# A two-layer hybrid trunk: the FFN up projection by seven quarter products, weight sums partly by accumulating DMAs, SBUF pools per sub-layer, adaLN sums moved

## The chip, the cores and the metric

The kernel runs on one core of a Trainium2 chip. TensorE (PE) multiplies, VectorE (DVE) and ScalarE (ACT) do element-wise work, GpSimd (POOL) a little, and SyncE (SP) issues the DMAs. The metric is device time in microseconds of one execution, as the median of repeated runs. A profile is one execution taken by the hardware profiler; its engines' busy times, waits and order of events are what this document reads.

## The reference

Two layers, each with a token mixer and a feed-forward part, over 512 latent and 128 context tokens that share the weights. What matters here is the feed-forward half of a layer (D_MODEL 1024, D_FF 2816), and the adaLN modulation that feeds both halves:

```python
def adaln(cvec, w_mod, b_mod):
    m = jax.nn.silu(cvec) @ w_mod + b_mod
    return jnp.split(m[:, None, :], 6, axis=-1)

def conv_glu(h, w_up, conv, w_down):
    u, val = jnp.split(h @ w_up, 2, axis=-1)
    u = dwconv3(u, conv)
    return (jax.nn.gelu(u, approximate=True) * val) @ w_down

def trunk_layer(...):
    sh1, sc1, gt1, sh2, sc2, gt2 = mod
    ...
    h = rmsnorm(x, g2n) * (1 + sc2) + sh2
    x = x + gt2 * conv_glu(h, w_up, f_conv, w_down)
```

The outputs are the normed tokens of both groups and the keys and values of every layer.

## The kernel before

All activations lie with channels on the 128 partitions and the 640 tokens along the free axis, as two halves of 320 (256 latent and 64 context tokens each). Every large product is taken in float32r with both operands split in two: a high part that ScalarE casts and a low part that VectorE makes by subtraction (`split`, and `block` for weights, lines 114 to 129 and 148 to 150). A product then is high times high, high times low and low times high: three matmuls per 128 channels and half of the tokens (`gemm`, line 136).

`block` loads a weight block of 128 x 1024 (512 KB) through SyncE's queue into one of three `raw` buffers, and writes its parts into one of two `hi`/`lo` pairs, or into spare tiles. PSUM gives out pairs of banks (`mmps`): two of tag `mm` and one of tag `m3`, so three products can be in flight.

`feed_forward` (line 591) runs over 22 units per layer, in two parts of 11. A unit f takes 48 matmuls for its gate block, evacuates them to a padded tile, convolves it with three taps (`dwconv`: one ScalarE and two VectorE instructions, lines 293 to 295), applies GELU, takes 48 matmuls for its value block, multiplies (line 616) and splits the result. After a part the down projection (`project`) adds its share to the residual x, eight blocks of 66 products per half each. Units 0 to 2 lead: `leading` multiplies the first half of the tokens for three blocks before the second half, while `norm` (line 240) still makes the second half's operands.

The adaLN sums are taken on VectorE: `mod_block` (line 162) loads two pieces of 256 KB of `w_mod`, multiplies each by both conditions with an accumulator output (line 171) and adds them up (line 173). 24 of these blocks go beside the branch projections of layer 0, one after each of 24 steps, and 56 beside the FFN of layer 0, two after a unit (`aside`, which only places them behind another instruction).

A list scheduler of the framework sets the order on each engine when the program is built; each engine then works its queue strictly in that order, and waits by semaphores. Pools with a fixed number of buffers per tag make later users wait for earlier ones.

Of the kernel before, what the change touches and what calls it, by code (L numbers as in the profile page):

```python
# [37 lines left out]
KSPARE = (4, 4, 3)  # L38
FTAGS = [("yc", 8)] + [("g", 2)] * 2 + [("vm", 9)] * 9 + [("qk", 10)] * 10
# [6 lines left out]
PARTS = ((0, 11), (11, 22))  # L46
KSPLIT = (6, 5)
# [7 lines left out]
def hybrid_kernel(ctx: ExitStack, tc: tile.TileContext, a):  # L55
# [3 lines left out]
    wp = ctx.enter_context(tc.tile_pool(name="wp", bufs=1))  # L59
    act = ctx.enter_context(tc.tile_pool(name="act", bufs=1))  # L60
# [22 lines left out]

    count = [0]
# [3 lines left out]
    fturn = [0]  # L88
# [5 lines left out]

    def big(tag, bufs, dt=F32):
        return act.tile([P, N], dt, tag=tag, bufs=bufs, name=uid(tag))

    def tmp(dt=F32, width=N):
        t = act.tile([P, PPW], dt, tag="tmp", bufs=NTMP, name=uid("tmp"))
# [14 lines left out]
    def block(src, n=1024, spare=None):  # L114
        """spare: places (first column, end, tag and bufs of both parts) for when the rotating ones are all held."""
        raw = wp.tile([P, 1024], F32, tag="raw", bufs=NRAW, name=uid("raw"))
        nc.sync.dma_start(raw[:, :n], src)
        parts = []
        if spare is None:
            hi = wp.tile([P, 1024], F32R, tag="hi", bufs=NW, name=uid("hi"))  # L120
            lo = wp.tile([P, 1024], F32R, tag="lo", bufs=NW, name=uid("lo"))
            parts.append((0, n, hi, lo))
# [30 lines left out]
    def load_cond():  # L153
        out = []
        for name in ("c", "c_ctx"):
            t = act.tile([P, 1152], F32, tag="bm", bufs=2, name=uid("cond"))[:, :D]
# [5 lines left out]
    def mod_block(l, i, cond):  # L162
        acc = sm.tile([P, 2, 2], F32, tag="macc", name=uid("macc"))
        for hf in range(2):
            turn[0] += 1
            tag, w = (("pt", 768), ("kc", 512), ("pt", 768), ("vca", 512))[turn[0] % 4]
            raw = act.tile([P, w], F32, tag=tag, bufs=2 if tag == "pt" else 1, name=uid("mraw"))[:, :512]
            nc.sync.dma_start(raw, a["w_mod"][l, i, :, hf * 512:(hf + 1) * 512])
            for s in range(2):
                scr = big("yt", 1)  # L170
# [25 lines left out]
    def rsqrt(st, v, r, t):  # L196
        """r = 1 / sqrt(st / D + EPS), with a Newton step"""
# [7 lines left out]
    def rstd(x, c, n=1):  # L205
        """1 / rms of the tokens of n halves from c on, the same on all partitions: one PSUM bank per half."""
# [17 lines left out]
    def half_tiles(n=2):  # L224
        t = act.tile([P, 768], F32, tag="pt", bufs=2, name=uid("xr"))
# [43 lines left out]
    def leading(n, src, h):  # L269
        """The first products after a norm: each half of the tokens for n blocks before the next half."""  # L270
# [95 lines left out]
    def softmax(s_ps, w, bias):  # L366
        s = act.tile([P, 384], F32, tag="s", bufs=4, name=uid("s"))
# [13 lines left out]
    def attention(l, qs, ks, vb, vc):  # L381
        kc = act.tile([P, 512], F32, tag="kc", bufs=1, name=uid("kc"))
        nc.sync.dma_start(kc, a["kc"][l].rearrange("p t n -> p (t n)"))
        vca = act.tile([P, 512], F32, tag="vca", bufs=1, name=uid("vca"))
# [4 lines left out]
        def behind(ins):  # L389
            """The products with V of the unit before: TensorE comes to them a little later than they could start."""  # L390
# [4 lines left out]
        def unit(t, j, bms):  # L395
            pt = act.tile([P, 768], F32, tag="pt", bufs=2, name=uid("pt")).rearrange("p (b e q) -> p b e q", b=3, e=2)
# [33 lines left out]
        def context(t):  # L430
            pt = act.tile([P, 768], F32, tag="pt", bufs=2, name=uid("pt")).rearrange("p (b e q) -> p b e q", b=3, e=2)
# [22 lines left out]
        for t in range(4):  # L454
            bms = []
            for e in range(2):
                bm = act.tile([P, 1152], F32, tag="bm", bufs=2, name=uid("bm")).rearrange("p (v n) -> p v n", v=3)
# [63 lines left out]
    def aside(ins, side, n):  # L521
        """The next n pieces of work that nothing waits for yet, behind ins."""
# [6 lines left out]
    def branch(l, b, h, ys, merged, last=False, side=[], between=None):  # L529
        parts = []  # L530
        for mp in range(4):
            if between:
                between(mp)
            for mi in range(2):
# [18 lines left out]
                aside(ins, side, 1)  # L553
        return parts

# [10 lines left out]
    def project(l, x, get, part, xt, n_last, side=[]):  # L566
        """x += gate * (W^T xt); the last n_last blocks finish one half of the tokens before the other."""
        for m in range(KD - n_last):
            ps = mmps()
            gemm(ps, get(m), xt)  # L570
            aside(residual(l, x, ps, m, part), side, 2)
# [12 lines left out]
    def ffn_block(src, n=1024):  # L584
        fturn[0] += 1
        if fturn[0] % 3:
            return block(src, n)
        y = ("yc", 8)
        return block(src, n, [(0, 512, y, y), (512, n, y, y)])

    def feed_forward(l, x, h):
        lead = leading(NLEAD, lambda i: a["w_up"][l, i], h)
        side = []
# [172 lines left out]
    for l in range(L):  # L766
        x, rb = layer(l, x, rb)
# [117 lines left out]
```

## Time and profile before

| | us |
|---|---|
| median of three runs | 2156.16 (2154.4 to 2160.48) |
| span of the profiled execution | 2153.5 |
| TensorE busy | 2114.8, 14280 matmuls |
| VectorE busy | 1116.8 |
| ScalarE busy | 723.3 |
| GpSimd busy | 100.6 |

The profile gives the span only, from the first to the last instruction; what lies around it is in the median's 2.7 us more. In the page each engine has its busy time and share; the groups of instructions give a mean duration per shape, and what ended the idle time before them. Matmuls overlap, so a matmul's own duration is about twice the pitch at which they follow each other.

### The profile page before, as it was taken

The numbers are of one execution on the slowest core, as the hardware profiler recorded it, in microseconds if no ns is written. First come the engines' busy times: TensorE is split into PE (matmuls) and PEld (weight loads), VectorE is DVE, ScalarE is ACT, GpSimd is POOL, SyncE is SP. The second block draws the span as 40 slices with busy tenths as digits, with TensorE's granted clock in tenths as the row PEclk, the third lists the DMA queues.
The fourth block names the chain that finished last, engine by engine and source line by source line (L and its number), as shares of the span: only waits on it lengthen the run. The fifth ranks groups of instructions, "written<-read, shape, count | busy, mean of one in ns | idle before, by whom it ended". The sixth has DMA issues, their size and how long they took to land.

```text
span 2153.5 us, 34873 instructions
## 1 busy us (share of the span) xinstructions
PE 2114.8 (98%) x14280; PEld 2038.5 (95%) x14280; DVE 1116.8 (52%) x2265; ACT 723.3 (34%) x1194; POOL 100.6 (5%) x300
## 2 busy tenths in 40 slices
PE   6999999999999999999999999999999999999998
PEld 4977999999999999999998779999999999999997
DVE  4247555556568778786352565323344643334434
ACT  4235432222354321333242452322223533123321
POOL 1001000000020000000020100000000200000000
PEclk9999999999999999999999999999999999999999
DMA  8241323345424445453322312222233222222222
GB/s 299 74 127 51 111 90 128 118 128 153 142 78 157 151 135 187 155 159 118 128 72 81 117 51 92 73 73 75 91 100 95 69 70 64 83 89 69 70 61 76
DMA packets 92032, 229.38 MB, mean 107 GB/s; under 512 B 10593, under 2 KB 20321, under 8 KB 91873
## 3 DMA queue, kind: packets, MB, share of 16 engines
q1 hardware_dynamic: 91872, 227.16, 33.4%
q8 instruction: 112, 1.84, 0.3%
q14 instruction: 48, 0.39, 0.1%
HBM read 216.10 MB, written 6.29 MB: 103 GB/s over the span
## 4 chain that ended last, share of the span: by engine, by line
PE 93%; DVE 3%; ACT 1%; POOL 1%; DMA 1%; issue 0%; SPq 0%; DVEq 0%; ACTq 0%; POOLq 0%
PE mm L141 60%; PE m L141 25%; PE ps L411 1%; PE ps L422 1%; PE m L401 1%; DVE h L150 1%; PE mm L346 1%; PE mm L344 1%; PE mm L345 1%; PE mm L732 1%; POOL xr L237 1%; POOL xr L234 0%; PE m L405 0%; DVE lo L128 0%; ACT h L149 0%
## 5 line engine op out<-in xcount | busy, mean ns | idle before, releaser
L141 PE MATMUL mm<-h,hi 128*128 128x320 f32 x3648 | 575.0, 310 | 1.0 <-ACT h L149 0.5
L141 PEld LDWEIGHTS mm<-h,hi 128*128 128x128 f32 x3648 | 542.2, 188 | 8.4 <-issue 2.1
L128 DVE TENSOR_TENSOR lo<-raw,hi 128x1024 fp32r<-128x1024 f32 (+1 forms) x240 | 278.8, 1162 | 367.8 <-PE mm L141 173.3
L127 ACT CAST hi<-raw 128x1024 fp32r<-128x1024 f32 (+1 forms) x240 | 240.5, 1003 | 585.0 <-PE mm L141 363.2
L141 PE MATMUL mm<-h,lo 128*128 128x320 f32 x1824 | 294.5, 310 | 0.0
L141 PEld LDWEIGHTS mm<-h,lo 128*128 128x128 f32 x1824 | 272.8, 188 | 3.4 <-issue 1.4
L171 DVE SCALAR_TENSOR_TENSOR yt<-mraw,cond 128x512 f32<-128x512 f32 x320 | 219.9, 687 | 5.4
L141 PE MATMUL m<-h,hi 128*128 128x320 f32 x1152 | 183.4, 311 | 4.1 <-ACT h L149 3.8
L141 PEld LDWEIGHTS m<-h,hi 128*128 128x128 f32 x1152 | 172.1, 188 | 8.7 <-ACT h L149 5.8
L128 DVE TENSOR_TENSOR yc<-raw,yc 128x512 fp32r<-128x512 f32 (+3 forms) x98 | 61.0, 624 | 130.0 <-ACT yc L127 72.8
L141 PE MATMUL mm<-vm,hi 128*128 128x320 f32 x626 | 113.1, 309 | 0.0
L141 PE MATMUL mm<-h,yc 128*128 128x320 f32 x672 | 100.9, 309 | 0.5 <-ACT tmp L608 0.5
L141 PE MATMUL m<-h,yc 128*128 128x320 f32 x672 | 100.9, 309 | 0.0
L141 PEld LDWEIGHTS mm<-h,yc 128*128 128x128 f32 x672 | 99.1, 188 | 0.7 <-ACT tmp L608 0.7
L141 PEld LDWEIGHTS m<-h,yc 128*128 128x128 f32 x672 | 99.1, 188 | 0.3 <-ACT tmp L608 0.3
L141 PEld LDWEIGHTS mm<-vm,hi 128*128 128x128 f32 x626 | 97.2, 188 | 0.4 <-DVE vm L150 0.4
L127 ACT CAST yc<-raw 128x512 fp32r<-128x512 f32 (+3 forms) x98 | 53.2, 565 | 130.0 <-DMA raw<-in_w_down 86.1
L141 PE MATMUL m<-h,lo 128*128 128x320 f32 x576 | 90.6, 308 | 0.0
L141 PEld LDWEIGHTS m<-h,lo 128*128 128x128 f32 x576 | 86.1, 188 | 0.0
L141 PE MATMUL mm<-yc,hi 128*128 128x320 f32 x370 | 75.4, 309 | 0.0
L141 PE MATMUL mm<-qk,hi 128*128 128x320 f32 x436 | 68.6, 309 | 0.0
L141 PEld LDWEIGHTS mm<-qk,hi 128*128 128x128 f32 x436 | 65.1, 188 | 0.0
(240 smaller groups left out, 2675.6 us busy)
## 6 DMA issues: line engine op xcount, KB each, us to landing
raw<-in_w_in SPq DMA_DIRECT2D x96, 512.0 KB, 3.6
raw<-in_w_up SPq DMA_DIRECT2D x88, 512.0 KB, 3.6
mraw<-in_w_mod SPq DMA_DIRECT2D x160, 256.0 KB, 2.9
raw<-in_w_branch SPq DMA_DIRECT2D x24, 512.0 KB, 3.5
raw<-in_w_down SPq DMA_DIRECT2D x30, 384.0 KB, 3.1
raw<-in_w_down SPq DMA_DIRECT2D x30, 320.0 KB, 2.9
raw<-in_w_out SPq DMA_DIRECT2D x16, 512.0 KB, 3.6
bm<-in_bias SPq DMA_DIRECT2D x16, 384.0 KB, 4.0
```

Of the source, the lines that this page charges most:

```text
L127: nc.scalar.copy(hi[:, :c1 - c0], raw[:, c0:c1])
L128: lows[0] = nc.vector.tensor_tensor(lo[:, :c1 - c0], raw[:, c0:c1], hi[:, :c1 - c0].bitcast(F32), ALU.subtract)
L141: nc.tensor.matmul(ps[:, c, :HALF], lhsT=w, rhs=v[:, c * HALF:(c + 1) * HALF], start=first, stop=last)
L150: return nc.vector.tensor_tensor(lo, src, hi.bitcast(F32), ALU.subtract)
L171: nc.vector.scalar_tensor_tensor(scr[:, :512], raw, 1.0, cond[s][:, hf * 512:(hf + 1) * 512], ALU.mult, ALU.mult, accum_out=acc[:, s, hf:h ...
L237: nc.gpsimd.tensor_scalar(t[:, HL:], t[:, HL:], sc[:, 1:2], sh[:, 1:2], ALU.mult, ALU.add)
L344: nc.tensor.matmul(o, lhsT=xh[:, tok], rhs=wh, start=(k == 0), stop=False)
L345: nc.tensor.matmul(o, lhsT=xh[:, tok], rhs=wl, start=False, stop=False)
L346: nc.tensor.matmul(o, lhsT=xl[:, tok], rhs=wh, start=False, stop=(k == KD - 1))
L401: nc.tensor.matmul(sps[:, e, 0:256].rearrange("p (r c) -> p r c", c=32), lhsT=qs[t][hs, j * P:(j + 1) * P], rhs=kb, start=True, stop=True)
L411: ins = nc.tensor.transpose(tp[:, b * P:(b + 1) * P], s[:, b * P:(b + 1) * P], ident)
L422: nc.tensor.matmul(y[e * 64:e * 64 + 64, 0:P], lhsT=v[:, t * P + e * 64:t * P + e * 64 + 64], rhs=pt[:, b, e, :], start=(b == 0), stop=(b ...
```

## The change

The up projection of a unit is a 2 x 2 block product: the channels in even and odd tiles (four each), the output in gate and value, the tokens in two halves. `seven` computes it as Strassen's scheme in Winograd's form does, by seven products M1 to M7 of 4 channel tiles x 3 = 12 matmuls, where one of the weights or operands is a sum of quarters. Two banks serve a unit, a and c: M1 on a is snapped to SBUF by ScalarE; M2 on c; M6 is added onto a and snapped again; M5 on c, snapped; M7 is added onto a, M3 onto c, M4 onto a. VectorE combines banks and snaps: gate of the first half after M2, value of the second half after M7 (L760), gate of the second half after M3, value of the first half after M4 (L767).

The weights come as four quarters of 512 columns, three of them in one load of 768 KB. Four sums of quarters are needed. Two are made by a load of 512 KB into `st` and an accumulating DMA from GpSimd's queue that adds the fourth quarter to both; the two others by VectorE (L636, L637). All seven weights are then split, 3584 columns instead of 2048 a unit, into three `hi`/`lo` pairs; `st` and `raw` have two buffers. `norm_quarters` makes the operands once per layer: two raw ones from the first half, five sums and raw ones that need the second.

The FFN has three parts, of 8, 8 and 6 units, each followed by a down projection with its own loads. SBUF comes from a pool for each sub-layer (`Stage`). The adaLN blocks are gone from the FFN: layer 0's branch stage now holds 48 of them, two after each of the 24 steps, and layer 1's 32.

```diff
-PARTS = ((0, 11), (11, 22))
-KSPLIT = (6, 5)
+PARTS = ((0, 8), (8, 16), (16, 22))
+NG = 16
...
-                aside(ins, side, 1)
+                aside(ins, side, (len(side) + 23 - left[0]) // (24 - left[0]))
+                left[0] += 1
...
+    def load_sums(src):
+        st = own([P, 2048], F32, "st", 2, "st")
+        nc.sync.dma_start(st[:, 512:1536], src[:, 512:1536])
+        nc.gpsimd.dma_start(st[:, 512:1536].rearrange("p (b n) -> p b n", b=2),
+                            src[:, 1536:2048].unsqueeze(1).to_broadcast([P, 2, 512]), accum_op=ALU.add)
+        return st
...
+    def sums_block(raw, st, out):
+        if not out:
+            split_quarters(out, raw[:, 0:1024], (2, 1))
+        q = [raw[:, i * 512:(i + 1) * 512] for i in range(3)]
+        s4, s3, s1, s2 = (st[:, i * 512:(i + 1) * 512] for i in range(4))
+        nc.vector.tensor_tensor(s2, s1, q[1], ALU.add)
+        nc.vector.tensor_tensor(s4, s2, q[0], ALU.add)
+        for t, ps in ((st[:, 1024:2048], (5, 6)), (st[:, 0:1024], (3, 7)), (q[2], (4,))):
+            split_quarters(out, t, ps)
+        return out
...
+        def product(p, o, fresh):
+            for j, (wi, xi) in enumerate(((0, 0), (1, 0), (0, 1))):
+                for k in range(NP):
+                    nc.tensor.matmul(o, lhsT=w[p][wi][:, k * P:(k + 1) * P], rhs=xt[k][p][xi],
+                                     start=fresh and j == 0 and k == 0, stop=j == 2 and k == NP - 1,
+                                     skip_group_check=not fresh)
+        def one():
+            product(1, a_, True)
+            kept[1] = snap(a_)
+        def two():
+            product(2, c_, True)
+            c11(c_, kept[1])
+        def six():
+            product(6, a_, False)
+            kept[2] = snap(a_)
+        def five():
+            product(5, c_, True)
+            kept[5] = snap(c_)
+        def sev():
+            product(7, a_, False)
+            c22(a_, kept[5])
+        def three():
+            product(3, c_, False)
+            c12(c_, kept[2])
+        def four():
+            product(4, a_, False)
+            c21(a_)
...
-        lead = leading(NLEAD, lambda i: a["w_up"][l, i], h)
+        xt = norm_quarters(x, l, 1, rb)
...
+        cond = load_cond()
+        side = mods(l, range(16, 48), cond) + (mods(l + 1, range(16), cond) if l + 1 < L else [])
```

What the scheduler makes of it, at three places. First VectorE in the middle of the FFN. Before, a unit there is (`yc`, `lo`: low parts of weights; L616: gate times value; L294, L295: taps; `vm`: low part of the result):

```order
L616 TENSOR_TENSOR tmp_2916_19234<-mm_2915_19185,tmp_2911_19174 128x2x256
L616 TENSOR_TENSOR tmp_2916_19234<-mm_2915_19185,tmp_2911_19174 128x2x64
L128 TENSOR_TENSOR lo_2936_19376<-raw_2934_19373,hi_2935_19375 128x1024
L150 TENSOR_TENSOR vm_2918_19238<-tmp_2916_19234,vm_2917_19237 128x640
L128 TENSOR_TENSOR lo_2942_19442<-raw_2940_19439,hi_2941_19441 128x1024
L294 SCALAR_TENSOR_TENSOR tmp_2924_19302<-tmp_2923_19296,vecs_75,tmp_2924_19302 128x642
L128 TENSOR_TENSOR yc_2951_19506<-raw_2947_19501,yc_2950_19505 128x512
L295 SCALAR_TENSOR_TENSOR tmp_2924_19302<-tmp_2923_19296,vecs_75,tmp_2924_19302 128x642
L128 TENSOR_TENSOR yc_2970_19702<-raw_2968_19699,yc_2969_19701 128x512
L616 TENSOR_TENSOR tmp_2931_19366<-mm_2930_19317,tmp_2924_19302 128x2x256
L616 TENSOR_TENSOR tmp_2931_19366<-mm_2930_19317,tmp_2924_19302 128x2x64
```

Now, from the last use of one `st` buffer (`st_1289`) to the first use of the next but one (`st_1329`, which takes the same place); L767 and L770 multiply the unit before, L755 sums the gate of the one that runs, L636 and L637 sum weights two units ahead, `lo_1311` is the low part for M1 and M2 of the next unit:

```order
L171 TENSOR_TENSOR lo_1295_7143<-st_1289_7129,hi_1294_7142 128x1024
L767 SCALAR_TENSOR_TENSOR tmp_1285_7118<-mm_1279_7016,tmp_1284_7113 128x256
L767 SCALAR_TENSOR_TENSOR tmp_1285_7118<-mm_1279_7016,tmp_1284_7113 128x64
L770 TENSOR_TENSOR tmp_1285_7118<-v_1283_7085,tmp_1284_7113 128x256
L770 TENSOR_TENSOR tmp_1285_7118<-v_1283_7085,tmp_1284_7113 128x64
L171 TENSOR_TENSOR lo_1297_7147<-raw_1288_7127,hi_1296_7146 128x512
L755 TENSOR_TENSOR tmp_1298_7150<-mm_1299_7154,sn_1300_7167 128x256
L171 TENSOR_TENSOR gs_1287_7124<-tmp_1285_7118,gs_1286_7123 128x640
L755 TENSOR_TENSOR tmp_1298_7150<-mm_1299_7154,sn_1300_7167 128x64
L636 TENSOR_TENSOR st_1329_7405<-st_1329_7405,raw_1328_7403 128x512
L637 TENSOR_TENSOR st_1329_7405<-st_1329_7405,raw_1328_7403 128x512
L171 TENSOR_TENSOR lo_1311_7271<-raw_1308_7265,hi_1310_7270 128x1024
```

Weight sums, gate sums out of PSUM and two products more per unit have come into the queue, and the weight sum on the accumulated buffer stands nine rows behind the row that frees that buffer.

Second, GpSimd's queue in the FFN of layer 1 before, which only clears the edges of the padded tiles:

```order
L281 MEMSET tmp_2661_16855 128x1
L282 MEMSET tmp_2661_16855 128x2
L283 MEMSET tmp_2661_16855 128x1
L281 MEMSET tmp_2670_16928 128x1
L282 MEMSET tmp_2670_16928 128x2
L283 MEMSET tmp_2670_16928 128x1
```

And now, in the FFN of layer 0:

```order
L302 MEMSET tmp_1278_7012 128x1
L303 MEMSET tmp_1278_7012 128x2
L304 MEMSET tmp_1278_7012 128x1
L619 DMA st_1309_7267<-in_w_up 128x2x512
L302 MEMSET tmp_1298_7150 128x1
L303 MEMSET tmp_1298_7150 128x2
L304 MEMSET tmp_1298_7150 128x1
L619 DMA st_1329_7405<-in_w_up 128x2x512
```

An accumulating DMA has come between the clearings of one unit and of the next.

Third, TensorE now, from the end of M7 of one unit (bank pair `mm_1279`) through the first seven matmuls of M1 of the next (`mm_1299`) to the start of M3:

```order
L656 MATMUL mm_1279_7016<-hT_1175_6398,hi_1274_7004 128x320
L656 MATMUL mm_1279_7016<-hT_1180_6413,hi_1274_7004 128x320
L656 MATMUL mm_1299_7154<-hT_1144_6301,hi_1290_7132 128x320
L656 MATMUL mm_1299_7154<-hT_1147_6312,hi_1290_7132 128x320
L656 MATMUL mm_1299_7154<-hT_1150_6323,hi_1290_7132 128x320
L656 MATMUL mm_1299_7154<-hT_1153_6334,hi_1290_7132 128x320
L656 MATMUL mm_1299_7154<-hT_1144_6301,lo_1291_7133 128x320
L656 MATMUL mm_1299_7154<-hT_1147_6312,lo_1291_7133 128x320
L656 MATMUL mm_1299_7154<-hT_1150_6323,lo_1291_7133 128x320
L656 MATMUL mm_1279_7016<-hT_1167_6374,hi_1274_7004 128x320
L656 MATMUL mm_1279_7016<-hT_1170_6383,hi_1274_7004 128x320
L656 MATMUL mm_1279_7016<-hT_1183_6422,hi_1274_7004 128x320
```

Before, the 48 matmuls of a block followed each other; now seven of the next unit's M1 stand between M7 and M3, three of them with the low part of the new weights.

## Rows read from the trace of the kernel before

**Rows 1.** The page: busy us, share of the span, instructions of each engine.

```profile
PE 2114.8 (98%) x14280; PEld 2038.5 (95%) x14280; DVE 1116.8 (52%) x2265; ACT 723.3 (34%) x1194; POOL 100.6 (5%) x300
```

**Rows 2.** Busy us of each engine by stretch, granted clock, DMA share, GB/s.

```profile
330.00:596.00 266.00, 266.00 (x1815) 265.81 (x1814) 155.37 (x308) 72.13 (x83) 0.00 (x0) 1.00 0.42 133
612.00:640.00 28.00, 26.31 (x165) 23.48 (x165) 21.07 (x48) 15.88 (x32) 14.14 (x27) 1.00 0.18 57
660.00:1069.00 409.00, 408.61 (x2786) 408.61 (x2787) 308.22 (x736) 127.14 (x198) 7.91 (x64) 1.00 0.47 151
1690.00:2120.00 430.00, 430.00 (x2933) 429.75 (x2932) 166.13 (x237) 138.65 (x212) 3.30 (x60) 1.00 0.24 74
```

**Rows 3.** The chain that ended last, FFN of layer 1: start, us, what.

```profile
1773.29 7.04 PE m L141 x48
1780.33 14.08 PE mm L141 x96
```

**Rows 4.** VectorE by line and shape: busy us, mean ns, idle before.

```profile
...
L128 DVE TENSOR_TENSOR lo<-raw,hi 128x1024 fp32r<-128x1024 f32 x198 | 241.4, 1220 | 319.8 <-PE mm L141 142.4 <-PE m L141 70.5 <-issue 56.7
...
L171 DVE SCALAR_TENSOR_TENSOR yt<-mraw,cond 128x512 f32<-128x512 f32 x320 | 219.9, 687 | 5.4
...
L295 DVE SCALAR_TENSOR_TENSOR tmp<-tmp,vecs,tmp 128x642 f32<-128x642 f32 x52 | 47.6, 916 | 2.2
...
L294 DVE SCALAR_TENSOR_TENSOR tmp<-tmp,vecs,tmp 128x642 f32<-128x642 f32 x52 | 45.9, 884 | 15.9 <-ACT tmp L293 15.7
...
L171 DVE DVE_READ_ACCUMULATOR yt<-mraw,cond 128x1 f32 x320 | 26.0, 81 | 0.0
...
L150 DVE TENSOR_TENSOR vm<-tmp,vm 128x640 fp32r<-128x640 f32 x24 | 19.7, 820 | 4.6 <-ACT vm L149 4.6
...
L173 DVE SCALAR_TENSOR_TENSOR mod<-macc,vecs 128x2 f32<-128x2 f32 x80 | 17.5, 218 | 1.9
...
L616 DVE TENSOR_TENSOR tmp<-mm,tmp 128x128 f32<-128x128 f32 x30 | 8.4, 280 | 0.0
...
L773 DVE SCALAR_TENSOR_TENSOR h<-mx,vecs,ps 128x320 f32<-128x320 f32 x16 | 7.7, 541 | 2.1 <-PE ps L219 2.1
...
L562 DVE SCALAR_TENSOR_TENSOR mx<-mm,mod,mx 128x256 f32<-128x256 f32 x14 | 6.7, 481 | 11.4 <-PE mm L141 11.3
...
L506 DVE TENSOR_TENSOR tmp<-tmp,tmp 128x512 f32<-128x512 f32 x8 | 5.5, 687 | 11.2 <-DMA tmp<-in_inv_cnt 11.2
...
L562 DVE SCALAR_TENSOR_TENSOR mx<-mm,mod,mx 128x64 f32<-128x64 f32 x14 | 3.8, 274 | 0.0
...
L128 DVE TENSOR_TENSOR yc<-raw,yc 128x256 fp32r<-128x256 f32 x8 | 3.4, 423 | 17.8 <-PE mm L141 14.2 <-PE m L141 3.6
...
```

**Rows 5.** ScalarE by line and shape, same columns.

```profile
...
L127 ACT CAST hi<-raw 128x1024 fp32r<-128x1024 f32 x198 | 207.6, 1050 | 511.9 <-PE mm L141 320.0 <-PE m L141 140.5 <-PE mm L346 18.1
...
L293 ACT ACTIVATE tmp<-tmp,vecs 128x642 f32<-128x642 f32 x52 | 43.3, 833 | 16.4 <-DVE tmp L476 11.2 <-issue 2.2
...
L610 ACT ACTIVATE tmp<-tmp 128x642 f32<-128x642 f32 x44 | 32.6, 741 | 89.6 <-DVE tmp L295 89.6
...
L149 ACT CAST vm<-tmp 128x640 fp32r<-128x640 f32 x24 | 17.5, 728 | 30.6 <-DVE tmp L616 30.4
...
L692 ACT COPY rb<-ps 128x320 f32<-128x320 f32 x2 | 0.9, 426 | 3.6 <-PE ps L219 3.6
...
```

**Rows 6.** DMA issues: queue, count, KB each, median us from issue to landing.

```profile
...
raw<-in_w_up SPq DMA_DIRECT2D x88, 512.0 KB, 3.6
...
mraw<-in_w_mod SPq DMA_DIRECT2D x160, 256.0 KB, 2.9
...
```

**Rows 7.** VectorE in order of time, FFN of layer 1: start, us, what.

```profile
1745.23 0.89 DVE L616 TENSOR_TENSOR tmp<-mm,tmp 128x512 f32<-128x512 f32 x2 [2.92 <-PE mm L141]
```

**Rows 8.** Stretches of 4 us near the start, columns as in rows 2.

```profile
28.00:32.00 4.00, 1.26 (x6) 0.61 (x5) 2.77 (x4) 2.83 (x6) 0.00 (x0) 0.97 1.05 386
32.00:36.00 4.00, 4.00 (x17) 4.00 (x18) 4.00 (x9) 0.58 (x1) 0.52 (x1) 0.50 1.05 388
```

More of the change, by code (lines that the diff above doesn't have):

```diff
@@ L82, in hybrid_kernel, with __init__, __enter__, __exit__ @@
     xs = dram.tile([P, KD, N], F32, name="xs")
+    pools, stage = [], []
+    class Stage:
+        def __init__(self, name):
+            self.name = name
+            self.guard = tc.tile_pool(name=uid(name), bufs=1, reuse_waits="tile")
+        def __enter__(self):
+            stage.append(self.name)
+            pools.append(self.guard.__enter__())
+        def __exit__(self, *args):
+            stage.pop()
+            pools.pop()
+            return self.guard.__exit__(*args)
     count = [0]
@@ L87, in hybrid_kernel @@
     busy = [False]
-    fturn = [0]
     lows = [None]
@@ L526, in aside, with branch @@
         del side[:n]
-    def branch(l, b, h, ys, merged, last=False, side=[], between=None):
+    def branch(l, b, h, ys, merged, left, last=False, side=[], between=None):
         parts = []
@@ L570, in project @@
             gemm(ps, get(m), xt)
-            aside(residual(l, x, ps, m, part), side, 2)
+            aside(residual(l, x, ps, m, part), side, 1)
         if n_last:
@@ new lines, in snap, with seven @@
+    def snap(src):
+        t = short("sn")
+        nc.scalar.copy(t, src)
+        return t
+    def seven(w, xt, ps, c11, c22, c12, c21):
+        a_, c_ = ps[:, 0, :HALF], ps[:, 1, :HALF]
+        kept = {}
+        def product(p, o, fresh):
[25 more added lines that the diff above has]
+            c21(a_)
+        return [one, two, six, five, sev, three, four]
@@ L635, in feed_forward @@
-            assert f1 < KF or not side
-            rb = project(l, x, wdown, 5, gs, 2 if f1 == KF else 0, side)
+                    steps, got = lead[f]
+                    sums_block(raws[0] if f == 0 else load_quarters(a["w_up"][l, f]), load_sums(a["w_up"][l, f]), ws[f])
+                else:
+                    steps, got = up(f)
+                for step in steps:
+                    step()
+                gs.append(finish(got))
+            n = f1 - f0
+            last = f1 == KF
+            def wdown(m, i=0):
+                raw = own([P, 1536], F32, "raw", 2, "raw")[:, :n * P]
+                nc.sync.dma_start(raw, a["w_down"][l, m, :, f0 * P:f1 * P])
+                hi, lo = own([P, 1024], F32R, "hi", 3, "hi"), own([P, 1024], F32R, "lo", 3, "lo")
+                split(raw, hi[:, :n * P], lo[:, :n * P])
+                return [cols([(0, n * P, hi, lo)], k) for k in range(n)]
@@ L637, in feed_forward @@
+            rb = project(l, x, wdown, 5, gs, 2 if last else 0)
         return rb
@@ L646, in mods, with mixer @@
         return [do(i) for i in idx]
-    def layer(l, x, rb):
+    def mixer(l, x, rb):
         if l == 0:
```

232 lines of the change are left out of this document (148 added, 84 removed).

## The prediction

> **What bounds the kernel now.** I read the busy shares of the page first: TensorE is busy for 98% of the span [rows 1]. Then the stretches one by one [rows 2]: in the branch stage of layer 0 and in the FFN of either layer TensorE is busy for all but 0.4 us of 1105 us, at a granted clock of 1.00 (the level of 2.4 GHz), while VectorE has 58%, 75% and 39%. The chain of waits gives the pitch: 48 matmuls of 128x320 last 7.04 us and 96 last 14.08 us [rows 3], so one matmul costs 146.7 ns, and one unit of the up projection (a gate block and its value block, 96 matmuls) costs 14.08 us. There are 44 units. So time is matmuls times 146.7 ns wherever TensorE never waits; the change matters by how many matmuls it takes away and by whether the other queues still keep up.
>
> **What it removes.** A unit has 7 products of 12 matmuls, 84 instead of 96: 12 x 44 = 528 matmuls, 77.4 us at most; a unit would take 12.32 us. The three-part down projection keeps its matmuls; its 8 more pairs of residual sums per layer are those of the two parts before once more, beside products of 7.04 us each: nothing.
>
> **What a unit now costs on VectorE.** Prices from [rows 4]: three subtractions for the low parts of 1024 columns (1.22 each) and one of 512 (0.69), two weight sums of 512 (0.69 each, by the row of that shape), the two convolution taps (0.88, 0.92), four sums out of PSUM that write the gate half by half (256 and 64 columns twice: 0.42 by the row of 256, 0.21 from the step between 256 and 128), the value sum of 320 (0.54), four products (0.48, 0.27, 0.42, 0.21) and the low part of the result (0.82). That is 11.5 us beside 12.3 us of matmuls. ScalarE's casts, snaps and activations come to 7.4 us with [rows 5] (a cast of 512 taken as 0.62, above half of one of 1024). Both fit, if the order of the queue never makes one wait for what stands far behind it. It does, so I walk one round of the order shown above, from one unit to the next.
>
> **The loop through the accumulating DMA.** There are two `st` buffers. VectorE's last use of one, the low part of sums 3 and 7 (first row of the VectorE piece), frees it; SyncE then loads 512 KB into it, GpSimd's queue issues the accumulating DMA, and the sum at L636 waits for that, nine rows further down. Behind L636 on VectorE stand the low part for the first products of the next unit, the value sum that frees a PSUM bank, and the gate sums; TensorE's product 3 waits for the value sum. The round, term by term: load 3.6 us [rows 6]; accumulation x; two weight sums 0.69 + 0.69; low part 1.22; value sum 0.54; product 3, 12 x 0.147 = 1.76; cast of the next 1024 columns, whose slot product 3 frees, 1.05 [rows 5]; its low part 1.22; taps 0.88 + 0.92; the low part that frees the buffer 1.22. Without load and x that is 10.2 us, so a round takes 13.8 us + x.
>
> The trace of before has no accumulating DMA and none from GpSimd's queue, so x is bounded by [rows 6]. From below: the HBM source is 256 KB, read twice, and a plain load of 256 KB takes 2.9. From above: reading the destination, adding and writing it one after the other is two plain loads of 512 KB, 7.2. I take 5.0: a plain 512 KB load, 3.6, plus two steps of 0.7 (what 256 KB more costs between the two rows) for the 512 KB that are read back. The round is then 18.8 us, 4.7 us longer than a unit before.
>
> The Trainium skill ("DMA: Bandwidth & Descriptors", Anatomy of one DMA — SWDGE (gpsimd) path) gives a transfer from GpSimd's queue as about 2.0 us plus its bytes at 436 GB/s, which I make an estimate of 3.2 us for 512 KB; by it the round would be 17.0 us and the sum below about 2291. It speaks of plain transfers, and no run here shows one yet.
>
> **The loop without it.** If the accumulation were always early, another round stays: cast 1.05, then on VectorE one after the other low part 1.22, taps 1.80, low part 1.22, products 1.39, low part 0.69, gate sum 0.42, result's low part 0.82, second gate sum 0.21; only then may product 5 overwrite its bank (1.76), ScalarE snaps it (0.43) and casts the next weights into the slot that product 5 freed (1.05), low part 1.22, value sum 0.54, product 3 1.76. Sum 15.6 us. Even this is longer than 14.08 us.
>
> **The sum per layer.** In the order, 11 of the 22 units have the accumulation in their round: 11 x 4.7 = +51.9. The last two of each of three parts have only the second loop: 6 x 1.5 = +9.1. The first unit of parts two and three finds its weights ready, since the down projection before it hides them: five products 8.8, less the overlap, to the end of product 3 12.1, twice -2.0 = -4.0. At each part's end come product 4 (1.76) and a wait for the last result: gate sums, one low part, taps, gelu, products, cast and low part are 8.2 us after product 3, against product 4 and 28 matmuls of the down projection, 5.9: 2.3 us. Three times 4.1 = +12.2. The lead: after the first half of the operands is there, VectorE has 43 instructions of 320 to 1024 columns, 23.6 us, for the second half's sums, differences and splits, against 72 matmuls of which 6 us are left; then units 0 to 2 cost it 36.8 us and some 11 us of waits for load and accumulation, against 26.4 us of matmuls. Neighbours that don't depend on each other overlap by some 0.08 us (a pair with means of 0.69 and 0.28 lasts 0.89 [rows 7]), some 7 us over these 90 instructions. With 4 us before, 4 + 23.6 + 36.8 + 11 - 7 is about 69 us for three units; before they took 42.2 us and some 5 us around the norm (153 full matmuls in 28.0 us there [rows 2]): +22. In all +91.2 a layer, 182.4 for two.
>
> **The adaLN sums.** One block costs VectorE 4 x (0.69 + 0.08) + 0.22 = 3.3 us [rows 4]. In the FFN of layer 0 VectorE loses 56 of them, 185 us, but TensorE never waited there: 0. Branch stage, layer 0: 48 blocks instead of 24, so 155.4 + 79 = 234 of 266 us; covered on the mean, but in the last 8 steps it is 1.83 + 1.64 + 0.82 + 6.6 = 10.9 us against 72 matmuls, 10.56: 8 x 0.34 = +2.7. SyncE's queue gets two more 256 KB loads a step, each waiting for a freed buffer ahead of the weight loads; I bound that by 0 and 10 us and take nothing, since layer 0's FFN issued as many per unit without a gap. Layer 1: 32 blocks where there were none, 76 + 106 of 266 us: nothing. The pools per sub-layer make the first FFN load wait for w_out's last slots; that is in the lead's margin (0 to 3 us).
>
> The profiled execution has a span of 2153.5 us; the median of the three runs, 2156.2, is 2.7 above. 2153.5 + 182.4 + 2.7 + 2.7 = 2341 us.
>
> **The rivals.** (1) Faster: the queues run ahead enough that TensorE is never held. For it: 11.5 us of VectorE and 7.4 of ScalarE beside 12.32, and VectorE at 75% held nobody in layer 0's FFN. Against it: both loops. It decides where a round falls below 14.08 us, for which x would have to be under 0.3 us and the second loop 1.5 us shorter. Then 2156.2 - 77.4 + 20 for the two leads + 3 = 2102. (2) The accumulation is hidden, the second loop stays: 11 x 3.2 and 11 us of the lead less per layer, 2341 - 92 = 2249. (3) TensorE's clock falls in the gaps. In a round of 18.8 us TensorE is idle for some 6 us, over 3.5 of it at a stretch before product 3. The trace shows one such place: from 28 to 32 us TensorE was busy 1.26 of 4 us, and at 32 the granted clock went to 0.50 (1.2 GHz) and stayed there to 36 [rows 8]. At that level product 3 takes 1.8 us more, and the 17 matmuls that the next cast waits for 2.5 more, some 0.3 of it slack: 4 us in 22 rounds, 2341 + 88 = 2429. The Trainium skill ("TensorE: Matmul & The Clock Gate", Part 1: The HAM clock gate) says the same in general: half the pulses after idling, all of them after sustained work; its reading of thin loops that fall every time is this rival.
>
> **How the numbers follow.** Forecast 0.60, clock 0.20, second loop alone 0.13, faster 0.05, no change 0.02. x between 2.9 and 7.2 moves 14 waits a layer, 28 us per us: 2282 to 2403. Rivals 2 and 3 widen that: down to 2235 (the second loop alone, and its round 0.4 us shorter in 34 units), up to 2457 (the clock falls and x is 6.0). What a measurement can tell from no change is about 0.3% (6.5 us). Slower 0.93, within 0.02, faster 0.05.
>
> **What would show it.** After: the FFN stretches with TensorE busy about two thirds; the largest wait on VectorE is L636 for the accumulating DMA on `st`, 2 to 5 us each; TensorE's waits are for L171 (low part), L760 and L755; product 3 starts every 18 to 19 us inside a part; granted clock near 1.00 in the FFN. Wrong if L636 hardly waits (the second loop), if the issue-to-landing time of `st` from GpSimd's queue is outside 2.9 to 7.2 us, if the clock in the FFN is well below 1.00, or if rounds are near 12.3 us.

## The result, and the profile after

The changed kernel takes **2533.1 us** (median of 4 runs, 2528.5 to 2536.1), the kernel before 2157.3 in the same comparison: ratio **1.1746, 95% interval 1.1726 to 1.1767**, slower by 17%. The forecast was 2341 with a range to 2457: the right direction, but half the size. The profiled execution has a span of 2534.3 us, 380.8 more than before.

Two rows of the page, busy us and share of the span by engine and the granted clock in 40 slices. TensorE falls from 98% [rows 1] to 87%, and the clock (in tenths of full speed) falls in the FFN:

```profile
PE 2215.2 (87%) x13752; PEld 2087.0 (82%) x13752; DVE 1353.6 (53%) x2747; ACT 804.6 (32%) x1261; POOL 167.1 (7%) x344
...
PEclk9999999999888978989999999999987889879889
```

The unit ends (first product of a result, L767) cut the FFN of layer 0 into pieces. Stretches of the trace after, columns as in [rows 2] (length, busy us of PE, PEld, DVE, ACT, POOL, clock, DMA share, GB/s): lead to the end of unit 2, rounds of part 1, first boundary (down projection of part 1 and first unit of part 2), rounds of part 2, rounds of part 3, and the mixer of layer 1:

```profile
620.50:708.20 87.70, 54.63 (x288) 49.69 (x288) 62.94 (x118) 40.48 (x63) 25.73 (x32) 0.79 0.41 108
708.20:816.00 107.80, 82.72 (x428) 76.88 (x429) 48.98 (x88) 33.77 (x49) 6.93 (x20) 0.81 0.35 91
816.00:894.60 78.60, 71.58 (x462) 69.67 (x460) 30.01 (x47) 16.08 (x20) 1.39 (x4) 0.96 0.24 71
894.60:1048.00 153.40, 116.66 (x596) 108.49 (x597) 69.63 (x123) 47.86 (x69) 9.72 (x28) 0.81 0.34 88
1127.00:1234.80 107.80, 80.25 (x421) 74.78 (x422) 48.18 (x88) 33.27 (x49) 4.52 (x18) 0.84 0.25 66
1275.80:1866.60 590.80, 577.77 (x3888) 547.84 (x3888) 339.05 (x739) 198.93 (x342) 37.91 (x69) 0.99 0.35 113
```

The same stretch of before as the first of these, the lead:

```profile
618.90:668.10 49.20, 47.17 (x306) 44.42 (x306) 34.50 (x76) 24.77 (x43) 12.06 (x29) 1.00 0.27 86
```

A round is the time from one unit's end to the next. So 17 rounds a layer (5 + 7 + 5) take 369.0 us, **21.7 us each**, against 14.08 before [rows 3]; and the granted clock in them is 0.81 to 0.84. With layer 1 cut in the same way:

| part, us more than before | forecast | layer 0 | layer 1 |
|---|---|---|---|
| lead, units 0 to 2 | +22 | +38.5 | +41.6 |
| 17 rounds (11 with, 6 without accumulation) | +61.0 | +129.6 | +128.5 |
| first units and part ends | +8.2 | +14.9 | +13.9 |
| mixer ahead of that FFN | +2.7, 0 | +1.6 | +11.2 |

With 1.0 at the very end that is the 380.8.

The waits of the trace after (who waited in which line for whom: us in total, times, longest):

```profile
DVE st L636 <- DMA st<-in_w_up: 235.3, 32, 8.9
PE mm L656 <- DVE tmp L755: 94.6, 29, 4.4
PE m L656 <- DVE tmp L755: 50.2, 15, 4.6
PE mm L656 <- ACT sn L644: 30.7, 58, 1.4
```

The first is the one foretold, but 7.4 us each instead of 2 to 5. The other three were not foretold as they are. One round in order of time shows why. TensorE, products 6, 5 and 7 of a unit, and VectorE beside them (start, us, what; in brackets the idle time ahead and what ended it):

```profile
897.53 1.44 PE L656 MATMUL mm<-hT,hi 128*128 128x320 f32 x4 [3.68 <-DVE tmp L755]
898.76 1.27 PE L656 MATMUL mm<-hT,lo 128*128 128x320 f32 x4
899.83 1.27 PE L656 MATMUL mm<-hT,hi 128*128 128x320 f32 x4
901.61 1.43 PE L656 MATMUL mm<-hT,hi 128*128 128x320 f32 x4 [0.52 <-ACT sn L644]
...
905.69 1.44 PE L656 MATMUL mm<-hT,hi 128*128 128x320 f32 x4 [0.52 <-ACT sn L644]
```

```profile
897.25 0.23 DVE L755 TENSOR_TENSOR tmp<-mm,sn 128x64 f32<-128x64 f32 x1
905.32 0.69 DVE L636 TENSOR_TENSOR st<-st,raw 128x512 f32<-128x512 f32 x1 [7.84 <-DMA st<-in_w_up]
906.04 0.69 DVE L637 TENSOR_TENSOR st<-st,raw 128x512 f32<-128x512 f32 x1
906.65 1.22 DVE L171 TENSOR_TENSOR lo<-raw,hi 128x1024 fp32r<-128x1024 f32 x1
909.30 0.49 DVE L760 SCALAR_TENSOR_TENSOR v<-mm,sn 128x320 f32<-128x320 f32 x1 [1.43 <-PE mm L656]
```

Product 6 starts only when the second part of the gate sum (64 columns, at 897.25) has ended, though that sum reads the other bank of the unit's PSUM tile; product 5 waits for the snap of 6, product 7 for the snap of 5, again of the other bank. The matmuls between these rows take 0.27 us each (four from 898.76 to 899.83), against 0.147 [rows 3]: the clock is at 1.2 GHz here.

The DMA issues of the page (queue, count, KB, median us from issue to landing):

```profile
raw<-in_w_up SPq DMA_DIRECT2D x44, 768.0 KB, 5.2
st<-in_w_up SPq DMA_DIRECT2D x48, 512.0 KB, 3.6
st<-in_w_up POOLq DMA_DIRECT2D x44, 512.0 KB, 6.5
```

x, taken as 5.0 us and bounded by 2.9 and 7.2, is 6.5. The next turn of the first loop in order of time, SyncE's load, GpSimd's accumulation and VectorE's sum:

```profile
917.96 0.33 SPq L618 DMA_DIRECT2D st<-in_w_up  x1
...
922.09 1.21 POOL L619 DMA_DIRECT2D st<-in_w_up  x1 [21.72 <-DMA st<-in_w_up]
...
929.51 0.69 DVE L636 TENSOR_TENSOR st<-st,raw 128x512 f32<-128x512 f32 x1 [8.84 <-DMA st<-in_w_up]
```

The load needs 3.6 us, so 0.5 lies between its landing and GpSimd's issue, and this accumulation takes 7.4 (a raw load of 768 KB, issued at 919.50, runs beside it).

### The profile page after: what moved, and what is told of

The parts are those of the page before. It is cut to its first block, busy times and chain, and to the rows that moved or that the text cites. A ratio compares the mean times of both kernels' runs of the same rounds, so it can differ in the third digit from the quotient of the medians.

```text
span 2534.3 us, 34503 instructions
## 1 busy us (share of the span) xinstructions
PE 2215.2 (87%) x13752; PEld 2087.0 (82%) x13752; DVE 1353.6 (53%) x2747; ACT 804.6 (32%) x1261; POOL 167.1 (7%) x344
## 5 line engine op out<-in xcount | busy, mean ns | idle before, releaser
L656 PE MATMUL mm<-hT,hi 128*128 128x320 f32 x1624 | 370.8, 361 | 147.5 <-DVE tmp L755 94.6
L656 PEld LDWEIGHTS mm<-hT,hi 128*128 128x128 f32 x1624 | 302.5, 226 | 180.7 <-DVE tmp L755 101.0
L162 PE MATMUL mm<-h,hi 128*128 128x320 f32 x2336 | 375.0, 314 | 7.6 <-ACT hi L148 5.9
L162 PEld LDWEIGHTS mm<-h,hi 128*128 128x128 f32 x2336 | 350.0, 190 | 15.3 <-ACT hi L148 6.1
L656 PE MATMUL m<-hT,hi 128*128 128x320 f32 x840 | 195.2, 360 | 87.6 <-DVE tmp L755 50.2
L149 DVE TENSOR_TENSOR lo<-raw,hi 128x1024 fp32r<-128x1024 f32 x140 | 170.8, 1221 | 139.8 <-PE mm L162 59.1
L656 PEld LDWEIGHTS m<-hT,hi 128*128 128x128 f32 x840 | 156.4, 224 | 105.6 <-DVE tmp L755 51.4
L656 PE MATMUL mm<-hT,lo 128*128 128x320 f32 x812 | 185.2, 353 | 25.2 <-DVE lo L171 25.2
L656 PEld LDWEIGHTS mm<-hT,lo 128*128 128x128 f32 x812 | 155.1, 226 | 27.9 <-DVE lo L171 27.8
L636 DVE TENSOR_TENSOR st<-st,raw 128x512 f32<-128x512 f32 x44 | 30.3, 692 | 267.2 <-DMA st<-in_w_up 235.3
L162 PE MATMUL mm<-gs,hi 128*128 128x320 f32 x936 | 147.4, 310 | 0.0
```

What stands on the lines that cost most here:

```text
L149: lows[0] = nc.vector.tensor_tensor(lo[:, :c1 - c0], raw[:, c0:c1], hi[:, :c1 - c0].bitcast(F32), ALU.subtract)
L162: nc.tensor.matmul(ps[:, c, :HALF], lhsT=w, rhs=v[:, c * HALF:(c + 1) * HALF], start=first, stop=last)
L636: nc.vector.tensor_tensor(s2, s1, q[1], ALU.add)
L656: nc.tensor.matmul(o, lhsT=w[p][wi][:, k * P:(k + 1) * P], rhs=xt[k][p][xi], start=fresh and j == 0 and k == 0, stop=j == 2 and k == NP - ...
```

## Experiments

Part 2 of layer 0 (7 rounds, unit 8's end to unit 15's) is used to compare rounds. The first loop is the one through the accumulating DMA, the second the loop without it.

**Without the accumulation.**

```
-        nc.gpsimd.dma_start(st[:, 512:1536].rearrange("p (b n) -> p b n", b=2),
-                            src[:, 1536:2048].unsqueeze(1).to_broadcast([P, 2, 512]), accum_op=ALU.add)
```

> The changed kernel without its accumulating DMAs: the fourth quarter is never added to the sums 1 and 3, so the products 3, 5, 6 and 7 use wrong weights; everything else stands. Theory A (a round is load 3.6 + 0.6 + accumulation 6.5 to 7.4 + 12.6 on the engines, of which 2.4 are there because TensorE runs at 1.2 GHz for a good third of a round): without the DMA a round falls on the second loop, which in the changed kernel shows as the rounds of 19.5 us where no accumulation is due; 17 rounds a layer by 2.2 us, some 12 us of the lead: about 2440 us, clock in the FFN still below 0.9. Theory B (the clock falls only because TensorE waits for the accumulation): rounds of 15.6 us, clock near 1.00, about 2300. Theory C (the accumulation is hidden and the clock is the whole of it): 2534 within 10.

2453.0 us (ratio to before 1.1382, 1.1357 to 1.1406). Seven rounds in 144.0 us, 20.6 each, at a clock of 0.83:

```profile
874.10:1018.10 144.00, 111.92 (x596) 104.19 (x597) 69.83 (x124) 47.77 (x69) 1.16 (x21) 0.83 0.20 68
```

Theory A as put, though its 19.5 was low. B and C fall: the DMA accounts for 80 us, and a round of 20.6 us is there without it. TensorE's waits for the gate sum stay too, 129.8 us in all, for 144.8 in the changed kernel.

**A plain write in its place** (the same DMA without `accum_op`).

> The changed kernel with the DMA of GpSimd's queue writing over sums 1 and 3 instead of adding to them (same 512 KB, same queue, same waits; the sums are wrong). It measures what of the 6.5 us is the adding and what is the queue. If the adding is dear (reading the destination back): 3 to 4 us from issue to landing, rounds at the 19.5 us of the second loop, about 2450 us. If it is the queue and the source that is read twice: 6 to 6.5 us, 2520 to 2540.

2477.9 us (two executions), and from the page:

```profile
st<-in_w_up POOLq DMA_DIRECT2D x44, 512.0 KB, 5.2
```

Between the two cases: the adding costs 1.3 of the 6.5 us. The other 5.2 are the queue and the source that is read twice, which no run parts; a plain load of 512 KB by SyncE's queue took 3.6. Rounds are 21.1 us, not the 19.5 named for either case.

**All four sums on VectorE.**

```
-        nc.sync.dma_start(st[:, 512:1536], src[:, 512:1536])
-        nc.gpsimd.dma_start(... accum_op=ALU.add)
+        nc.sync.dma_start(st[:, 512:2048], src[:, 512:2048])
...
+        nc.vector.tensor_tensor(s3, s3, s2, ALU.add)
+        nc.vector.tensor_tensor(s1, s1, s2, ALU.add)
         nc.vector.tensor_tensor(s2, s1, q[1], ALU.add)
```

> No accumulating DMA: the fourth quarter is loaded in the same DMA as the second and third (768 KB, 5.2 us by the raw loads of the same size) into the place of sum 2, and VectorE makes all four sums (two more of 512 columns, 0.69 us each). Theory A: a round is 5.2 + 12.6 + 1.4 = 19.2 us by the first loop and 19.5 by the second (20.9 if the two more sums lie in it), against 21.7 on the mean: 2440 to 2500 us. Rival (VectorE is the bound and two more sums cost their time in every unit): 44 x 1.4 = 61 us more, 2595.

2467.4 us, inside the interval. Rounds of 21.1 us at 0.81, within 0.5 us of the run with nothing to wait for: VectorE has 79 of 147 us, so it isn't the bound, and something else holds a round near 20.6.

**Matmuls to keep the clock up**, 16 ahead of product 2 and 24 ahead of product 3.

> The changed kernel with 40 matmuls of 128x320 per unit that nobody reads, into a spare PSUM bank, 16 ahead of product 2 and 24 ahead of product 3, to keep TensorE busy in the waits (5.9 us at 2.4 GHz of some 9 us in which it would be idle at that level). Theory A: granted clock near 1.00 in the FFN, engines' part of a round 10.2 to 11 instead of 12.6, rounds of 20 to 21 us, 2440 to 2490 us. Rival (the clock is only a mark of the waits and costs nothing by itself): 2534 or, with the 40 matmuls in the way, above it.

2527.8 us: a miss. The clock did rise, the rounds stayed:

```profile
886.00:1039.30 153.30, 138.10 (x870) 133.54 (x870) 71.07 (x123) 48.63 (x69) 9.72 (x28) 0.96 0.35 88
```

21.9 us at 0.96. In the built order the matmuls were strewn between all products in pieces of 4 to 16, some of them in the way; and the loop through the accumulation stays: 13.8 us plus the measured 0.5 + 6.5 is 20.8, and L636 waits for the accumulation as long as before, 229.9 us in 32 waits for 235.3. How much of a round the strewn matmuls cost was not parted from that.

**Two tiles for the two banks.**

```
-        a_, c_ = ps[:, 0, :HALF], ps[:, 1, :HALF]
+        a_, c_ = ps
...
+            ps = mmps()
+            ps = ps[:, 0, :HALF], (ps[:, 1, :HALF] if f < NLEAD else smps()[:, :HALF])
```

> The changed kernel with the two PSUM banks of a unit as two tiles (from unit 3 of a layer on) instead of one tile of two banks. In the changed kernel each product waits for the reader of the product before, though that reads the other bank: product 6 for the second gate sum, 5 for the snap of 6, 7 for the snap of 5, 3 for the value sum, 4 for the gate sum. Theory D (this is the 2.4 us by which the second loop, 18.0 us at 2.4 GHz by the rounds of the run without accumulation, exceeds the 15.6 us of the prediction): the second loop falls to 15.6 and the rounds without accumulation (6 a layer) from 19.5 to 22 us to 16 to 18; the rounds with it stay at 20.9 us or more, since load, accumulation and VectorE's chain set them: 2470 to 2510 us. Rival (the weights are late and the banks hold nobody): 2533 within 10.

**2297.5 us** (1.0653, 1.0635 to 1.0671), 236 us less, where 23 to 63 were expected. The seven rounds take 15.5 us each, at a clock of 0.95, with the accumulation still there. The wait for it falls to a third of 235.3, and TensorE's waits for the gate sum fall from 144.8 us to 12.4:

```profile
856.90:965.60 108.70, 93.02 (x580) 89.35 (x581) 68.99 (x122) 47.60 (x69) 9.73 (x28) 0.95 0.46 123
```

```profile
DVE st L636 <- DMA st<-in_w_up: 79.1, 28, 4.6
```

The built order shows two more differences, which the scheduler made of the same edit: the weight sum L636 now stands behind the value sum and the low part for the next unit's first products, where in the changed kernel it stands ahead of both; and on TensorE product 7 goes ahead of product 5, which alone waits for the gate sum. So theory D named the wait, but not what its going would bring. Two runs below part the place of L636 from the rest; no run parts the order of products 7 and 5 from the two tiles.

**Two tiles and VectorE's sums**, then **two tiles and a third buffer for the sums**, to see what is left.

```
-PARTS = ((0, 8), (8, 16), (16, 22))
-NG = 16
+PARTS = ((0, 6), (6, 12), (12, 17), (17, 22))
+NG = 12
...
-        st = own([P, 2048], F32, "st", 2, "st")
+        st = own([P, 2048], F32, "st", 3, "st")
```

> Both: all four sums on VectorE after one plain load of 768 KB, and the two banks as two tiles. Theory A with D: first loop 5.2 + 10.2 + 1.4 = 16.8 us, second 15.6 to 17.0; rounds of 17 to 19 us against 20.7 with one tile: 17 rounds a layer, 2340 to 2400 us, and a granted clock in the FFN that is no lower. Rival (no more than the run with one tile): 2467.

> The accumulating DMAs stay, with three buffers for the sums instead of two (room for the third comes from four parts of 6, 6, 5 and 5 units instead of 8, 8 and 6), and the two banks as two tiles. Theory A with D: load and accumulation start a unit earlier and leave the round; what stays is the second loop of 15.6 us, 15 rounds a layer of 15.6 to 18 us, and one more part's end of some 7 us a layer: 2320 to 2400 us. Rival (the transfers slow each other down, or VectorE's queue is the bound whatever the buffers): above 2440.

2201.2 us (1.0209, 1.0194 to 1.0225) and 2205.0 us (1.0222, 1.0207 to 1.0237): both far better than expected, by either way of taking the accumulation out of the round. The rounds are shorter than the loop of 15.6 us, which the expectations had kept; with product 7 ahead of 5 that loop no longer runs as it was walked. The row of the first, 13.2 us a round, the clock at 1.00, VectorE busy for 84%:

```profile
836.10:928.60 92.50, 87.81 (x588) 85.97 (x587) 77.51 (x136) 48.48 (x69) 1.16 (x21) 1.00 0.36 125
```

**Order or tile.** The first is two tiles without accumulation, where the place of L636 has nothing to wait for; the second is one tile with the accumulation, and only the order changed:

```
+        with tc.issue_after(v.ins) if v else nullcontext():
             nc.vector.tensor_tensor(s2, s1, q[1], ALU.add)
             nc.vector.tensor_tensor(s4, s2, q[0], ALU.add)
```

> Without the accumulating DMAs (sums 1 and 3 stay unsummed, as in the run that left them out with one tile) and with the two banks as two tiles. It parts two readings of the run with two tiles: there VectorE's queue also changed, the weight sum that waits for the accumulation moved from ahead of the value sum to behind it. Without accumulation that place cannot matter. Theory D (the waits of one tile are the cause): rounds of 12.4 to 13.2 us, 2180 to 2205 us. Rival (the order did it): near the 2453 of the run without accumulation and one tile.

> The changed kernel with one edit of order: the two weight sums of a unit stand behind the value sum of the unit two before, as they do with two tiles; accumulation and the one tile stay. If the order is what the two tiles brought: 2297 us. Theory D: the wait for the accumulation leaves product 3's way, but the second loop of 18.0 us plus the clock's part stays, as without accumulation: 2450 to 2490 us, rounds of 19.5 to 22.

2203.6 and 2477.6 us, both as theory D has it. The rows (13.4 us a round, a little above the 12.4 to 13.2; 21.1):

```profile
833.90:927.70 93.80, 88.31 (x589) 86.04 (x588) 68.77 (x122) 48.20 (x70) 1.16 (x21) 1.00 0.30 103
```

```profile
886.80:1034.50 147.70, 115.57 (x596) 107.77 (x597) 69.58 (x124) 47.73 (x69) 9.73 (x28) 0.82 0.35 91
```

Without accumulation the two tiles, with the order of products 7 and 5 that the scheduler makes of them, are worth 249 us, and TensorE's waits for the gate sum go from 129.8 us to 1.7; the place of L636 alone is worth 56. In the run with the order VectorE hardly waited for the accumulation (L637 is L636 there), and the round was still 21 us: the one tile holds it.

```profile
DVE st L637 <- DMA st<-in_w_up: 25.0, 10, 4.2
```

**The clock by itself**, without accumulation, 24 matmuls exactly between products 2 and 6.

```
+            with tc.issue_after(last[0].ins):
+                for _ in range(24):
+                    nc.tensor.matmul(spin, lhsT=xt[0][1][0][:, :P], rhs=xt[0][1][0], start=True, stop=True)
             product(6, a_, False)
```

> Without the accumulating DMAs (sums 1 and 3 unsummed), one tile, and 24 matmuls of 128x320 per unit that nobody reads, exactly between product 2 and product 6, where TensorE waits 3.7 us for the second gate sum; 24 last 3.5 us at 2.4 GHz, so they delay nothing if the clock holds. The clock's own price: if each stretch at 1.2 GHz lengthens a round (18.0, 19.3, 20.5, 22.0, 23.3 us with none to four stretches of 3.4 us, the first worked out from the others), rounds fall from 20.5 to 18.0 to 18.5 us with a clock near 1.00, some 2.2 us in 34 rounds: about 2380 us. Rival (the clock marks waits and costs nothing): 2453; or more, if the matmuls stand in the way.

2376.6 us. Seven rounds in 126.2 us, 18.0 each, at a clock of 1.00, and one of them in order of time (TensorE, then VectorE; the 24 matmuls are L654, the products L660 in this kernel):

```profile
860.70:986.90 126.20, 117.89 (x759) 111.06 (x758) 69.55 (x124) 47.90 (x69) 1.16 (x21) 1.00 0.25 78
```

```profile
913.94 3.68 PE L654 MATMUL ps<-hT 128*128 128x320 f32 x24
917.79 0.85 PE L660 MATMUL mm<-hT,hi 128*128 128x320 f32 x4 [0.16 <-DVE tmp L760]
...
920.32 0.85 PE L660 MATMUL mm<-hT,hi 128*128 128x320 f32 x4 [0.52 <-ACT sn L642]
...
922.86 0.85 PE L660 MATMUL mm<-hT,hi 128*128 128x320 f32 x4 [0.52 <-ACT sn L642]
...
925.75 0.75 PE L660 MATMUL mm<-hT,hi 128*128 128x320 f32 x4
```

```profile
917.52 0.21 DVE L760 TENSOR_TENSOR tmp<-mm,sn 128x64 f32<-128x64 f32 x1
...
923.79 1.23 DVE L171 TENSOR_TENSOR lo<-raw,hi 128x1024 fp32r<-128x1024 f32 x1
924.93 0.48 DVE L765 SCALAR_TENSOR_TENSOR v<-mm,sn 128x320 f32<-128x320 f32 x1
```

1056 more matmuls made the kernel 76 us faster. The second loop at full clock is 18.0 us, and the lower level adds 2.6 us to a round between these two traces, 2.2 by the medians (the profiled execution without the matmuls was 8.6 us above its median).

**The adaLN sums moved alone**, in the kernel before.

```
-                aside(ins, side, 1)
+                aside(ins, side, (len(side) + 23 - left[0]) // (24 - left[0]))
+                left[0] += 1
```

> The kernel before with the adaLN sums moved alone: none in the FFN of layer 0, 48 blocks in the branch stage of layer 0 and 32 in that of layer 1; its FFN is the old one. By the prediction 2.7 us in the branch stage of layer 0 and nothing else: 2159 us. The traces of the two kernels have the first mixer 1.6 us longer and the second 11.2 us longer; if the move is the cause of both: 2169. If the pools per sub-layer or the FFN before it are the cause of the 11.2: 2158.

2156.5 us against 2156.5 (1.0003, 0.9993 to 1.0012): nothing. Its second mixer is 3.1 us longer and its FFN of layer 0 1.6 shorter by the same cuts, so most of the 11.2 us isn't the move. What the move does is in the attention: it lasts 109.6 us here and 109.0 in the changed kernel, for 102.5 before (first to last of its matmuls), but in both it holds 26 or 27 more matmuls of other products, and what follows it in the mixer is 4.2 us shorter. The other 9.0 us lie ahead of the attention (99.1 us for 90.1, and 90.1 with the move alone). Most of that is one wait for the first weights of the next mixer, which the kernel before does not have. Its row in the run with two tiles and VectorE's sums; in the changed kernel it is as long, at 1281.27:

```profile
1110.32 1.17 PE L162 MATMUL mm<-h,hi 128*128 128x320 f32 x3 [5.87 <-ACT hi L148]
```

The pools change at this place, which may be the cause; the pools alone were not tried. The same mixer lasts between 590.6 and 596.4 us in the changed kernel and three of the variants, so single microseconds of it say little.

**A shorter lead**, with two tiles and VectorE's sums: one unit in it instead of three.

> Two tiles and all four sums on VectorE, with one unit in the lead instead of three (all units with two tiles). In that kernel the lead is the dearest part left: 82 us to the end of unit 2 against 49 before, 15.6 us of it one wait of TensorE for the cast of the sums, which stand on VectorE behind all differences of the second half. If VectorE's work in the lead is the bound (70 of 83 us busy), fewer units in it only give less for TensorE to do meanwhile: 2201 to 2225 us. If the wait for slots and places in the queue is, unit 0 goes on sooner: 2175 to 2195.

2194.5 us (1.0179, 1.0164 to 1.0194), at the upper end of the second interval, 7 us better: the best of the variants of this scheme, and still 39 us behind the kernel before. Nothing tried beats that one. But the number came out by another path than the expectation's. Unit 0 does end sooner, 53.6 us into the lead for 60.7, and yet the end of unit 2 comes no sooner: the two leads last 84.1 and 80.3 us, with three units 82.8 and 81.3. The profiled executions differ in the mixer of layer 1 (590.6 for 596.4 us) and behind it, so what bounds the lead stays open. What the run with three units shows in the lead:

```profile
618.50:700.90 82.40, 55.99 (x305) 51.65 (x306) 69.29 (x130) 40.66 (x64) 18.62 (x27) 0.77 0.27 101
```

```profile
659.84 1.44 PE L656 MATMUL m<-hT,hi 128*128 128x320 f32 x4 [15.61 <-ACT hi L170]
```

VectorE is busy for 84% of it; before, the whole stretch lasted 49.2 us.

## Why the forecast was half the size

**What held.** The matmuls fell as said, by 528. In the FFN a loop of waits takes the place of matmul time, the largest wait of VectorE is L636 for the accumulating DMA, the adaLN sums cost nothing (1.6 us for 2.7), and the sign follows. x was inside its bounds.

**The step that failed: the loop without accumulation, 15.6 us.** It went from the second gate sum to product 5 at once, "only then may product 5 overwrite its bank", as if the two banks were two resources. In the built kernel they are one, by the tile: product 6 waits for that gate sum, 5 for the snap of 6, 7 for the snap of 5. From the gate sum's end to product 3 the forecast had 5.0 us (1.76 + 0.43 + 1.05 + 1.22 + 0.54); at full clock the trace has 917.73 to 925.75, 8.0. Product 6 and its snap, which the forecast hadn't put there, take 2.6 of them (917.73 to 920.32); from product 5 on it is 5.4, as product 7 runs beside the cast and the low part. The rest of the loop was right within 1 us (10.0 for 10.6), and 18.0 stands where 15.6 was written. The forecast has no wait of product 6 for the gate sum at all.

**The clock was a term, not a rival.** The forecast had "granted clock near 1.00 in the FFN", and a clock well below that as one of its signs of being wrong; in the rounds it is 0.81 to 0.84. Rival 3 gave the clock 4 us in 22 rounds, 88 us, at a chance of 0.20, on top of the loop through the accumulation. Measured without that loop, it is 76 us, 2.2 in each of 34 rounds. That the two totals are near each other is luck in part: the price was worked out for other products, in other rounds. TensorE waits for the gate sum ahead of product 6, 3.2 us on the mean of 40 waits without the accumulation and up to 4.1, and behind it runs at 1.2 GHz through product 6 and often 5 and 7, which stand in series, so the time goes straight into the loop. The 18.0 us become 20.6. That the Trainium skill ("TensorE: Matmul & The Clock Gate", Part 1: The HAM clock gate) expects idling to lower the clock in every turn of a thin loop agrees with these rows.

**The accumulation, 18.8 us a round, was under-sized, and not the bound alone.** With 0.5 + 6.5 for x it is 13.8 + 7.0 = 20.8 us, at full clock. So two loops of 20.8 and, with the clock as it falls, 20.6 us lie beside each other, and taking out one leaves the other: without accumulation 20.6 us, with the order changed 21.1, with the clock raised 21.9. Only the two tiles shorten both, since the built order then puts L636 behind the value sum too: 15.5. The Trainium skill ("DMA: Bandwidth & Descriptors", Anatomy of one DMA — SWDGE (gpsimd) path) led to an estimate of 3.2 us for a plain 512 KB; here the plain write, from a source read twice, took 5.2 and the adding one 6.5, and the measurement decides.

**What that makes of rival 2.** Accumulation hidden and the second loop alone was put at 2249; without the accumulation it is 2453. Of the 204 us, 76 are the clock (2453 to 2377), 82 are the 2.4 us in each of 34 rounds by which the loop is longer at full clock, the lead holds 45 (80.6 and 82.3 us for the two layers, +31 and +35, where that rival left +11 of the 22), and the second mixer 14 (593.5 us, for 579.6). The ends of the parts were 12 us cheaper than it had them; that makes 205, so nothing large is left without a place.

**The lead, +22, measured +38.5 and +41.6.** VectorE's work was 60.4 us in the forecast, some 53 with the overlaps, and is 62.9 busy of 87.7 in the whole stretch. What the forecast left out is that TensorE comes to a stand for the cast of the first sums, which stand behind all differences in VectorE's queue, and then runs at 1.2 GHz (the clock is 0.50 from 656 to 668 us, 0.79 on the mean of the lead):

```profile
659.54 1.44 PE L656 MATMUL m<-hT,hi 128*128 128x320 f32 x4 [14.24 <-ACT hi L170]
```

**Open.** Whether the pools cause the wait ahead of the second mixer, and what bounds the lead. What the order of products 7 and 5 is worth beside the two tiles. Whether the scheme can beat the kernel before was not settled: the best variant is 39 us behind, its two leads together are some 67 us longer than before, and its rounds (13.2 us) are already 0.9 us shorter.

## What to carry to other kernels

When you walk a loop by hand, take every wait by the tile that is declared, not by which bytes an instruction touches: two banks in one tile were one resource here, and making them two tiles, with the orders that came of it, was worth 236 us of 376. When two loops are of nearly the same length, taking out either shows little (80 and 56 us here), and both together show all; so judge a cause by pairs of runs. And a TensorE that waits a few us in every round can pay twice, once in the wait and once in the matmuls behind it: in the kernel without accumulation, matmuls that nobody reads, put exactly into the wait, bought 76 us; strewn between the products, in the kernel with it, they bought 5.

## What the chip showed that was not expected

An accumulating DMA of 512 KB from GpSimd's queue, its 256 KB source read twice, took 6.5 us from issue to landing (medians of 6.5 to 7.0 in the five kernels that have it), the plain write by the same queue 5.2, and a plain load of 512 KB by SyncE's 3.6. The engine's own time to issue one was 1.2 us, for 0.7 with the plain write:

```profile
L619 POOL DMA_DIRECT2D st<-in_w_up x44 | 53.1, 1207 | 995.6 <-DMA st<-in_w_up 995.6
```

The length of a round went with the clock it was granted. Two rounds of the run without accumulation took 19.3 and 20.5 us at 0.91 and 0.83; with the wait filled a round was 18.0 us at 1.00:

```profile
915.60:934.90 19.30, 14.59 (x84) 13.63 (x84) 10.36 (x20) 6.92 (x11) 0.17 (x3) 0.91 0.20 69
934.90:955.40 20.50, 15.85 (x84) 14.61 (x84) 10.30 (x19) 6.87 (x11) 0.16 (x3) 0.83 0.18 64
```
